# A two-layer attention and expert kernel: attention in two stages, float32r scores over 128 rows, weight splits moved from GpSimd

## Chip, core and metric

The kernel runs on one core of a Trainium2 chip. The metric is device time in microseconds (us) from the start of the program to its end. The engines are named as in the profile: PE is TensorE with its matmuls, PEld its weight loads, DVE is VectorE, ACT is ScalarE, POOL is GpSimd, SP is SyncE, whose queue issues the DMAs.

## What is computed

Two layers over 256 tokens of 1024 features. Layer 0 mixes tokens by a sparse attention with three branches (compressed, selected, window), layer 1 by a forgetting attention with a decay; each is followed by a product-key expert layer. Of the reference, cut to what matters here:

```python
# layer 0 (nsa): 16 heads of 64, 4 key groups; three branches, each gated
q = rope(proj[..., :1024]); k_slc, k_win = rope(kv[:, :, 2]), rope(kv[:, :, 4])
s_c = einsum(q, k_cmp); p_c = masked_softmax(s_c, cmp_end <= t)
s_s = einsum(q, ks);    p_s = masked_softmax(s_s, pos_s <= t)
s_w = einsum(q, kw);    p_w = masked_softmax(s_w, causal window)
o = g0 * (p_c @ v_cmp) + g1 * (p_s @ vs) + g2 * (p_w @ vw);  h = h + o @ w_out
# layer 1 (fox)
s = einsum(q, k) + c[t] - c[k]; p = masked_softmax(s, k <= t); h = h + (p @ v) @ w_out
# after each: h = h + peer_ffn(rms_norm(h)), whose first step is q = x @ w_q
```

With 256 tokens every block is selected and the window covers all, so selected and window attention are both plain causal attention, with keys of their own (branch b = 0, 1 in the kernel).

## The kernel before

A list scheduler sets the order of the instructions on each engine by the data they need and by costs; `pin` keeps a piece in program order, and `tc.issue_after(mark)` holds the ACT instructions written inside it back until ACT has issued the marked one. Each engine then runs its list in order.

Weights come in as float32 and are split into two float32r parts: `hi`, a cast on ACT (L116), and `lo`, a subtract (L117) on DVE or, where `eng` says so, on GpSimd. A projection is three matmuls per block, hi x hi, hi x lo and lo x hi (L200 to L202). `w_half` loads half a weight tile (4 blocks of 128 x 512) into a ring of three slots, by SP (L189); the compression network's weights w1 (L384) use slots of the same ring, so that a slot comes free for the next w_in load when the network's matmuls (L388) that read it are done.

`nsa` is layer 0. It projects the compressed key and value tokens, then k, then q in two tiles of 512 columns (`q_tile`), then v and the gates. k is rotated (`rope`, DVE L291 to L299), transposed on PE (L356) and copied to `kT` by ACT (L358). The token transposes L365 and the DVE adds L370 lay out the input of the compression network, whose matmuls L388 are spread between the matmuls of the q tiles. q is transposed at L430. Then come the compressed scores and softmax (L473 to L490), of which L490 are transposes on PE.

The rounds follow: eight, j = 0 to 7, a round for two heads and two branches. For each half of the tokens (qt) and each of the two heads (s) the scores of both branches go into one PSUM tile: a float32 matmul L508 over 64 rows (256 or 512 columns wide) and a bf16 matmul L509 that adds the causal mask through `identb` and `maskb`. DVE takes the maximum (L510), ACT the exponential (L512), DVE the sums' limit, reciprocal and gate (L513 to L516); the probabilities are scaled on DVE (L523) and ACT (L521), transposed on PE (L529), copied (L532), and multiplied with the values (L539, L540, and L544 for the compressed branch). ACT and DVE split the result (L546, L547), and ACT's cast is kept as `marks[j]`. In the code the values of round j stand right behind its scores.

`fox` is layer 1, with rounds of the same form: scores L641 (66 rows, float32), mask L642, maximum L643, exponential L645, L646 to L649 on DVE, transposes L654, copies L655 and L657, values L662 and L663.

`out_proj` multiplies with w_out in four halves. ACT casts of halves 0, 1 and 2 or 3 are held back to marks 0, 2, 4 (nsa) or 0, 3, 6 (fox); GpSimd subtracts for halves 0 to 2, DVE for half 3. `peer` is the expert layer: the query projection over 16 blocks of wq (`load_split`, L672; matmuls L689, L692, L693), then the long blocks of u and v.

Of the kernel before, what the change touches and what calls it, by code (L numbers as in the profile page):

```python
# [17 lines left out]
P = 128  # L18
S = 256
# [20 lines left out]
def body(ctx, tc, A, out):  # L40
# [12 lines left out]
    identb = const.tile([P, P], BF16, name="identb")  # L53
    maskb = const.tile([P, P], BF16, name="maskb")
# [170 lines left out]
    def out_proj(HL, w, oh, ol, gi, marks):  # L225
# [19 lines left out]
        mm(0, 1)  # L245
        add(0, 0)
        mm(0, 2)
        mm(0, 3)
        add(0, 1)
        mm(1, 1)  # L250
        add(1, 0)
# [8 lines left out]
    def nsa():  # L260
# [3 lines left out]
        TOK, XO, SO = 10240, 12288, 14336  # L264
        qT = ar(6144, 8, S)
        kT = ar(8192, 2, 2, S)
# [76 lines left out]
        for tt in range(2):  # L343
# [3 lines left out]
            for u in range(2):  # L347
                ACT.activation(t4[:, :, u], o[tt][:, 256:512].rearrange("p (g e) -> p g e", e=64), AF.Copy, scale=norm.rs[tt])

        o = proj_tok(HL, wsrc[512], 512, xh, xl)  # L350
        for tt in range(2):
            kf = t2k(4, P)
            rope(o[tt], 8, 1, tt, kf.rearrange("p b (u e) -> p (b u) e", u=2))
            pt = pst("g")
            for b in range(4):
                PE.transpose(pt[:, b * P:(b + 1) * P], kf[:, b], ident)  # L356

            ACT.copy(kT.rearrange("p g b t -> p b g t")[:, :, :, tt * P:(tt + 1) * P],  # L358
                     pt.rearrange("p (b g t) -> p b g t", b=2, g=2))
# [90 lines left out]
        V.reciprocal(gates, gates)  # L450
# [19 lines left out]
        for tt in range(2):  # L470
# [16 lines left out]
            pt = pst("g")  # L487
            pf = ar(XO + tt * 512, 4, P)
# [612 lines left out]
```

## Time and profile before

| | us |
|---|---|
| runs of before | 1962.12, 1963.22, 1964.39 (median 1963.22) |
| profiled execution | 1965.05 |
| its span, first to last instruction | 1962.9 |
| PE busy over the span | 1930.9 |
| DVE busy over the span | 1402.2 |
| ACT busy over the span | 987.4 |
| POOL busy over the span | 158.2 |

The span is 2.15 us shorter than the execution's own time; the rest lies around it. A matmul's busy time is longer than its share of PE, because matmuls overlap: the time from one start to the next is what one costs in a row of them. Layer 0's projections fill the span up to 87.5 us, the compressed softmax to 105.2, the rounds to 167.4, the output projection to 187.8 and the query projection of the expert layer to 240. Layer 1's rounds run from 1075 to 1123 us, its output projection to 1143.

### The profile page before, as it was taken

The page shows a single profiled execution, that of the slowest core. Times are in us where ns is not written, and L with a number is a line of the kernel's source. Part 1 is how long each engine was busy: PE and PEld are TensorE (multiplying, and loading weights), DVE is VectorE, ACT ScalarE, POOL GpSimd, SP SyncE. Part 2 cuts the span into 40 slices and gives each one's busy share as a digit, 9 for nine tenths or more (in the row PEclk, how much of TensorE's full clock was granted, in tenths as well). Part 3 has the DMA queues.
Part 4 walks back from the last instruction along what each step waited for, and adds up shares of the span by engine and source line. Part 5 has one row for each costly group of instructions (what it writes and reads, how often), then busy time and mean ns, then how long its engine had stood idle before and what let it go on. Part 6 is the DMA issues. An engine that isn't in the chain of part 4 may idle for free.

```text
span 1962.9 us, 34000 instructions
## 1 busy us (share of the span) xinstructions
PE 1930.9 (98%) x13091; PEld 1717.4 (87%) x13091; DVE 1402.2 (71%) x2984; ACT 987.4 (50%) x1870; POOL 158.2 (8%) x98
## 2 busy tenths in 40 slices
PE   9999999999999999999999999999999999999998
PEld 6747999999999888888879699999999998888886
DVE  8586998478888655555585779956788875555555
ACT  5564545555444544444463555455544444444444
POOL 4011600000000000000050252000000000000001
PEclk9999999999999999999999799999999999999999
DMA  7701555554545666666664235565454556666664
GB/s 294 262 28 65 162 163 184 181 163 159 157 156 162 223 217 215 192 194 194 194 229 146 70 106 160 174 190 170 159 162 151 162 169 194 194 216 203 194 194 140
DMA packets 90193, 340.91 MB, mean 174 GB/s; under 512 B 9872, under 2 KB 12336, under 8 KB 84656
## 3 DMA queue, kind: packets, MB, share of 16 engines
q1 hardware_dynamic: 89744, 338.22, 54.0%
q8 instruction: 103, 1.69, 0.3%
q10 hardware_dynamic: 288, 0.52, 0.1%
q14 instruction: 58, 0.48, 0.1%
HBM read 334.48 MB, written 4.19 MB: 173 GB/s over the span
## 4 chain that ended last, share of the span: by engine, by line
PE 79%; DVE 15%; ACT 3%; issue 2%; DMA 0%; POOL 0%; ACTq 0%
PE m L966 12%; PE m L965 12%; PE m L964 12%; PE h L692 9%; PE h L689 9%; PE h L693 9%; DVE lo L117 5%; ACT hi L116 2%; PE m L907 2%; PE m L200 2%; PE m L201 2%; PE m L202 2%; PE m L908 1%; PE m L508 1%; DVE vhl L900 1%
## 5 line engine op out<-in xcount | busy, mean ns | idle before, releaser
L117 DVE TENSOR_TENSOR lo<-raw,hi 128x1024 fp32r<-128x1024 f32 x512 | 628.5, 1228 | 397.1 <-ACT hi L116 393.8
L116 ACT CAST hi<-raw 128x1024 fp32r<-128x1024 f32 (+1 forms) x576 | 576.5, 1003 | 640.1 <-PE m L966 293.8
L693 PE MATMUL h<-xh,lo 128*128 128x256 f32 x2048 | 581.8, 284 | 2.1 <-DVE lo L117 2.1
L689 PE MATMUL h<-xh,hi 128*128 128x256 f32 x2048 | 580.6, 284 | 0.9 <-ACT E L925 0.9
L692 PE MATMUL h<-xl,hi 128*128 128x256 f32 x2048 | 580.4, 283 | 0.0
L965 PE MATMUL m<-lo,vhl 128*128 128x512 f32 x1024 | 398.7, 389 | 0.0
L966 PE MATMUL m<-hi,vhl 128*128 128x512 f32 x1024 | 398.7, 389 | 0.0
L964 PE MATMUL m<-hi,vhl 128*128 128x512 f32 x1024 | 398.7, 389 | 0.0
L693 PEld LDWEIGHTS h<-xh,lo 128*128 128x128 f32 x2048 | 386.5, 189 | 4.8 <-DVE lo L117 4.1
L689 PEld LDWEIGHTS h<-xh,hi 128*128 128x128 f32 x2048 | 386.5, 189 | 1.5 <-ACT E L925 1.3
L692 PEld LDWEIGHTS h<-xl,hi 128*128 128x128 f32 x2048 | 386.7, 189 | 0.0
L965 PEld LDWEIGHTS m<-lo,vhl 128*128 128x128 f32 x1024 | 192.4, 188 | 40.3 <-DVE lo L117 0.5
L966 PEld LDWEIGHTS m<-hi,vhl 128*128 128x128 f32 x1024 | 192.4, 188 | 39.9
L964 PEld LDWEIGHTS m<-hi,vhl 128*128 128x128 f32 x1024 | 192.3, 188 | 39.8
L117 POOL TENSOR_TENSOR E<-arena,E 128x1024 fp32r<-128x1024 f32 (+1 forms) x20 | 46.8, 2358 | 917.1 <-ACT E L116 904.0
L117 POOL TENSOR_TENSOR lo<-raw,hi 128x512 fp32r<-128x512 f32 x64 | 90.8, 1438 | 95.6 <-ACT hi L116 95.4
L916 ACT ACTIVATE arena<-m 128x256 f32<-128x256 f32 (+25 forms) x128 | 37.7, 303 | 79.9 <-DVE arena L914 75.9
L116 ACT CAST E<-arena 128x1024 fp32r<-128x1024 f32 (+2 forms) x68 | 62.5, 955 | 27.6 <-DMA arena<-in_w_in 14.4
L689 PE MATMUL h<-E,hi 128*128 128x256 f32 x240 | 70.3, 293 | 3.1 <-ACT arena L761 3.1
L117 DVE TENSOR_TENSOR E<-arena,E 128x1024 fp32r<-128x1024 f32 (+2 forms) x48 | 58.2, 1239 | 17.6 <-ACT E L116 17.5
L117 DVE TENSOR_TENSOR vhl<-E,vhl 128x512 fp32r<-128x512 f32 x64 | 44.1, 688 | 34.1 <-ACT vhl L116 34.1
L693 PE MATMUL h<-E,lo 128*128 128x256 f32 x240 | 68.1, 284 | 0.0
(281 smaller groups left out, 2519.1 us busy)
## 6 DMA issues: line engine op xcount, KB each, us to landing
raw<-in_u SPq DMA_DIRECT2D x256, 512.0 KB, 3.5
raw<-in_v SPq DMA_DIRECT2D x256, 512.0 KB, 3.8
arena<-in_w_in SPq DMA_DIRECT2D x18, 1024.0 KB, 5.0
raw<-in_wq SPq DMA_DIRECT2D x32, 512.0 KB, 3.7
arena<-in_w SPq DMA_DIRECT2D x8, 1024.0 KB, 6.4
arena<-in_w_out SPq DMA_DIRECT2D x8, 1024.0 KB, 5.0
hd<-arena SPq DMA_DIRECT2D x3, 1024.0 KB, 4.5
arena<-hd SPq DMA_DIRECT2D x3, 1024.0 KB, 5.2
```

Source lines behind the costliest of these rows:

```text
L116: ACT.copy(hi, raw)
L117: (eng or V).tensor_tensor(lo, raw, hi.bitcast(F32), ALU.subtract)
L200: PE.matmul(o[:, :n], sh[:, cc, tsl], wh[:, c], start=cc == 0, stop=False)
L201: PE.matmul(o[:, :n], sh[:, cc, tsl], wl[:, c], start=False, stop=False)
L202: PE.matmul(o[:, :n], sl[:, cc, tsl], wh[:, c], start=False, stop=cc == 7)
L689: t = PE.matmul(o[:, :S], hi[:, c % 4], sh[:, c], start=c == 0, stop=False)
L692: PE.matmul(o[:, :S], hi[:, c % 4], sl[:, c], start=False, stop=False)
L693: PE.matmul(o[:, :S], lo[:, c % 4], sh[:, c], start=False, stop=c == 7)
L907: PE.matmul(o, o2[:, k, :, u], oh[:, k, :, u], start=True, stop=False)
L964: PE.matmul(acc[tt][nh], gh[:, ts], vh, start=first, stop=False)
L965: PE.matmul(acc[tt][nh], gh[:, ts], vl, start=False, stop=False)
L966: PE.matmul(acc[tt][nh], gl[:, ts], vh, start=False, stop=last)
```

## The change

Three things change.

Layer 0's scores: `stacked` rotates q or k, splits it into hi and lo, lays both side by side so that a transpose gives 64 rows of hi and 64 of lo, and transposes (8 for each tile of 512 columns and half of the tokens). k is stored twice, hi over hi (`ks_`) and lo over zeros (`kl_`, zeroed by GpSimd), q as hi over lo (`qs_`). A score is then two float32r matmuls over 128 rows and a float32r mask (in fox the mask too). q is also transposed as before, for the compressed branch. These arrays lie in the buffers of the expert layer's weight stream (`ustr`), so that layer 0's wq blocks can't be loaded while they are read. The gates of the rounds are no longer inverted by themselves: one DVE instruction multiplies the limited sum with the gate's denominator, and one reciprocal follows.

Two stages: `weights_of(j)` holds scores, softmax and scaling, `values_of(j)` transposes and values, and round j+1's first is written ahead of round j's second, in both layers. The compressed branch's transposes (`turn_compressed`) stand behind `weights_of(0)`.

Splits: all halves of w_out are split by ACT and DVE, after marks 2, 5, 7; the first two halves' matmuls of both token halves go first. The first two wq blocks are split by ACT and DVE after marks[7], instead of by GpSimd at any time before; the other 14 stay on GpSimd.

```diff
...
-    identb = const.tile([P, P], BF16, name="identb")
-    maskb = const.tile([P, P], BF16, name="maskb")
+    identb = const.tile([P, P], F32R, name="identb")
+    maskb = const.tile([P, P], F32R, name="maskb")
...
-        half_in = lambda i: w_half(HL, w[i // 2][:, i % 2 * 4:i % 2 * 4 + 4, :], 512, (GP, GP) if i < 3 else (V, V))
+        half_in = lambda i: w_half(HL, w[i // 2][:, i % 2 * 4:i % 2 * 4 + 4, :], 512, (V, V))
         ws = []
+        mm = lambda tt, i: proj_mm(o[tt][i // 2], 512, i % 2, tt, oh, ol, *ws[i])
         for i in range(4):
             with tc.issue_after(marks[min(i, 2)]):
                 ws.append(half_in(i))
-            if i == 0:
+            if i < 2:
                 for tt in range(2):
-                    proj_mm(o[tt][0], 512, 0, tt, oh, ol, *ws[0])
+                    mm(tt, i)
...
-        mm(0, 1)
         add(0, 0)
+        add(1, 0)
         mm(0, 2)
         mm(0, 3)
         add(0, 1)
...
+        qs_ = [tl(ustr, t, [4, S], F32R, 3) for t in ("raw", "raw", "raw", "hi")]
+        ks_ = [tl(ustr, "hi", [2, 2, S], F32R, 3) for _ in range(2)]
+        kl_ = [tl(ustr, "lo", [2, 2, S], F32R, 3) for _ in range(2)]
         qT = ar(6144, 8, S)
-        kT = ar(8192, 2, 2, S)
...
+        def stacked(o, ti, tt, put):
+
+            f = t2k(8, 64)
+            rope(o, 8, ti, tt, f)
+            hl = t4k(8, 2, 64)
+            split(f, hl[:, :, 0].bitcast(F32R), hl[:, :, 1])
+            for q in range(2):
+                pt = pst("g")
+                for b in range(4):
+                    PE.transpose(pt[:, b * P:(b + 1) * P], hl[:, 4 * q + b].rearrange("p u e -> p (u e)"), ident)
+                put(q, pt.rearrange("p (b t) -> p b t", b=4))
+            return f
...
+        for x in kl_:
+            GP.memset(x[64:128].bitcast(F32), 0.0)
         o = proj_tok(HL, wsrc[512], 512, xh, xl)
         for tt in range(2):
-            kf = t2k(4, P)
-            rope(o[tt], 8, 1, tt, kf.rearrange("p b (u e) -> p (b u) e", u=2))
-            pt = pst("g")
-            for b in range(4):
-                PE.transpose(pt[:, b * P:(b + 1) * P], kf[:, b], ident)
-
-            ACT.copy(kT.rearrange("p g b t -> p b g t")[:, :, :, tt * P:(tt + 1) * P],
-                     pt.rearrange("p (b g t) -> p b g t", b=2, g=2))
+            def put_k(br, pt):
+                for g01 in range(2):
+                    src = pt[:, 2 * g01:2 * g01 + 2]
+                    to = lambda x: x[:, :, br, tt * P:(tt + 1) * P]
+                    ACT.copy(to(ks_[g01][0:64]), src[0:64])
+                    V.tensor_copy(to(ks_[g01][64:128]), src[0:64])
+                    (ACT.copy if g01 else V.tensor_copy)(to(kl_[g01][0:64]), src[64:128])
+
+            stacked(o[tt], 1, tt, put_k)
...
-                qf = t2k(4, P)
-                rope(o[tt], 8, 0, tt, qf.rearrange("p b (u e) -> p (b u) e", u=2))
+                ts = slice(tt * P, (tt + 1) * P)
+                f = stacked(o[tt], 0, tt, lambda q, pt: ACT.copy(qs_[2 * qi + q][:, :, ts], pt))
+
                 pt = pst("g")
                 for b in range(4):
-                    PE.transpose(pt[:, b * P:(b + 1) * P], qf[:, b], ident)
-                ACT.copy(qT[:, qi * 4:qi * 4 + 4, tt * P:(tt + 1) * P], pt.rearrange("p (b t) -> p b t", b=4))
+                    PE.transpose(pt[:, b * P:(b + 1) * P], f[:, 2 * b:2 * b + 2].rearrange("p u e -> p (u e)"), ident)
+                V.tensor_copy(qT[:, qi * 4:qi * 4 + 4, ts], pt.rearrange("p (b t) -> p b t", b=4))
...
-        V.reciprocal(gates, gates)
+        V.reciprocal(gates[:, :, 0:16], gates[:, :, 0:16])
...
+        def turn_compressed():
+            for tt in range(2):
...
+        def weights_of(j):
             g01, r = j // 4, j % 4
...
-                    PE.matmul(s3, qT[64 * s:64 * s + 64, j, qs], kT[64 * s:64 * s + 64, g01, :, :K], start=True, stop=False)
+                    qx = qs_[2 * g01 + r // 2][:, 2 * (r % 2) + s, qs]
+                    PE.matmul(s3, qx, ks_[g01][:, s, :, :K], start=True, stop=False)
+                    PE.matmul(s3, qx, kl_[g01][:, s, :, :K], start=False, stop=False)
                     PE.matmul(s3[:, :, K - P:K], identb, maskb.unsqueeze(1).broadcast_to((P, 2, P)), start=False, stop=True)
...
-                V.tensor_scalar(su, su, 1e-30, None, ALU.max)
+                gv = gates[:, qt, 16:48].rearrange("p (b r g) -> p g b r", b=2, r=4)[:, g01::2, :, r]
+                V.scalar_tensor_tensor(su, su, 1e-30, gv, ALU.max, ALU.mult)
                 V.reciprocal(su, su)
-                gv = gates[:, qt, 16:48].rearrange("p (b r g) -> p g b r", b=2, r=4)[:, g01::2, :, r]
-                V.tensor_tensor(su, su, gv, ALU.mult)
...
+            return Pts
+
+        def values_of(j, Pts):
+            g01, r = j // 4, j % 4
+            PT0 = ar(TOK + (j % 2) * 1024, 2, 2, S)
+            PT1 = t2k(2, 2, P)
+            for qt, Pt in enumerate(Pts):
...
+        held = weights_of(0)
+        turn_compressed()
+        for j in range(1, 8):
+            nxt = weights_of(j)
+            values_of(j - 1, held)
+            held = nxt
+        values_of(7, held)
         h_in(xsrc)
-        return out_proj(HL, A["w_out0"], oh, ol, 1, [marks[i] for i in (0, 2, 4)])
+        return out_proj(HL, A["w_out0"], oh, ol, 1, [marks[i] for i in (2, 5, 7)]), marks[7]
...
-        return out_proj(HL, A["w_out1"], oh, ol, 3, [marks[i] for i in (0, 3, 6)])
+        return out_proj(HL, A["w_out1"], oh, ol, 3, [marks[i] for i in (2, 5, 7)]), marks[7]
...
-        parts = [load_split(wq[b], (GP, GP)) for b in range(2)]
+        with tc.issue_after(mark):
+            parts = [load_split(wq[b]) for b in range(2)]
...
-    norm = peer(0, nsa())
-    peer(1, fox(norm))
+    norm = peer(0, *nsa())
+    peer(1, *fox(norm))
```

Where the order of instructions moves. On PE, in layer 0's projections, around the token transposes (L365 before, L383 after) and the first compression matmuls (L388, h_463 before; L406, h_511 after); m_432 is a sum of the first q tile, m_629 one of the second, g a PSUM tile of transposes. Before:

```order
L365 MATMUL g_404<-cst,arena 128x128 x2
L388 MATMUL h_463<-arena 15x128 x3
L200 MATMUL m_432<-E_85,xh 128x512
L388 MATMUL h_463<-arena 15x128 x2
L365 MATMUL g_411<-cst,arena 128x128 x2
L388 MATMUL h_463<-arena 15x128 x11
L201 MATMUL m_432<-E_85,xh 128x512
L365 MATMUL g_418<-cst,arena 128x128 x2
L202 MATMUL m_432<-E_85,xl 128x512
L200 MATMUL m_432<-E_85,xh 128x512
```

After:

```order
L406 MATMUL h_511<-arena 15x128 x3
L383 MATMUL g_459<-cst,arena 128x128 x2
L406 MATMUL h_511<-arena 15x128 x11
L383 MATMUL g_466<-cst,arena 128x128 x2
L406 MATMUL h_511<-arena 15x128 x12
L383 MATMUL g_473<-cst,arena 128x128 x2
L406 MATMUL h_511<-arena 15x128 x19
L360 MATMUL g_584<-cst,vhl_581 128x128 x4
L360 MATMUL g_590<-cst,vhl_581 128x128 x4
L200 MATMUL m_629<-E_85,xh 128x512
```

Before, matmuls of the first q tile alternate with both; after, they are all ahead, and the next projection matmul is the second q tile's, behind 8 more transposes of q (L360).

On PE, in layer 0's rounds, the scores (L508 and L509 before; L532, L533 and L534 after), the transposes of the probabilities (L529, L561) and the values (L571). Before:

```order
L508 MATMUL m_1286<-arena 128x512
L509 LDWEIGHTS identb
L509 MATMUL m_1286<-maskb,identb 128x2x128
L508 MATMUL m_1292<-arena 128x512
L529 MATMUL g_1229<-cst,vhl_1207 128x128 x4
L529 MATMUL g_1235<-cst,vhl_1207 128x128 x4
```

After:

```order
L534 MATMUL m_1263<-maskb,identb 128x256
L532 MATMUL m_1270<-hi_90,raw_87 128x256
L533 MATMUL m_1270<-lo_92,raw_87 128x256
L534 MATMUL m_1270<-maskb,identb 128x256
L532 MATMUL m_1286<-hi_90,raw_87 128x512
L533 MATMUL m_1286<-lo_92,raw_87 128x512
L534 MATMUL m_1286<-maskb,identb 128x2x128
L561 MATMUL g_1241<-cst,vhl_1127 128x128 x4
L571 MATMUL h_1247<-arena 64x256
L532 MATMUL m_1293<-hi_90,raw_87 128x512
```

Before, the transposes of g_1229 belong to the round of scores ahead of m_1286 and m_1292 (to m_1210 and m_1216); after, those of g_1241 belong to m_1130 and m_1137, two rounds ahead of m_1286, and each score has two float32r matmuls.

On DVE, in layer 1's rounds, the softmax multiplies (L649 before, L689 after) with sums' limit and reciprocal around them, and the split of a piece of w_out (L117). Before:

```order
L665 TENSOR_TENSOR E_10663<-h_11580,E_10663 128x256
L649 TENSOR_SCALAR vraw_11606<-vraw_11606,fsu_11608 128x256
L647 RECIPROCAL fsu_11637<-fsu_11637 128x2
L646 TENSOR_SCALAR fsu_11655<-fsu_11655 128x2
L646 TENSOR_SCALAR fsu_11684<-fsu_11684 128x2
L649 TENSOR_SCALAR vraw_11635<-vraw_11635,fsu_11637 128x128 x2
L647 RECIPROCAL fsu_11655<-fsu_11655 128x2
L647 RECIPROCAL fsu_11684<-fsu_11684 128x2
```

After:

```order
L689 TENSOR_SCALAR vraw_11749<-vraw_11749,fsu_11751 128x256 x2
L686 TENSOR_SCALAR fsu_11784<-fsu_11784 128x2
L686 TENSOR_SCALAR fsu_11798<-fsu_11798 128x2
L683 TENSOR_REDUCE fnm_11830<-m_11832 128x2
L687 RECIPROCAL fsu_11784<-fsu_11784 128x2
L687 RECIPROCAL fsu_11798<-fsu_11798 128x2
L117 TENSOR_TENSOR E_10783<-arena,E_10783 128x1024
L713 TENSOR_TENSOR E_10783<-h_11775,E_10783 128x256
L689 TENSOR_SCALAR vraw_11782<-vraw_11782,fsu_11784 128x128 x2
L689 TENSOR_SCALAR vraw_11796<-vraw_11796,fsu_11798 128x256 x2
L705 COPY vhl_11810<-g_11815 128x256
L686 TENSOR_SCALAR fsu_11831<-fsu_11831 128x2
```

Before, no split of w_out stands in the piece; after, the first one of that layer stands ahead of the multiplies of sums fsu_11784 and fsu_11798.

## Rows read from the trace of the kernel before

**Rows 1.** Stretch, length; busy us (instructions) by engine; PE's clock; DMA share, GB/s.
```profile
0.00:87.50 87.50, 83.57 (x586) 63.06 (x586) 61.26 (x137) 44.06 (x86) 23.74 (x17) 0.98 0.80 284
105.20:167.40 62.20, 61.47 (x337) 33.17 (x335) 47.10 (x126) 39.39 (x138) 14.04 (x6) 0.97 0.12 39
167.40:187.80 20.40, 20.40 (x98) 16.94 (x97) 10.36 (x31) 7.85 (x21) 0.00 (x0) 1.00 0.16 52
187.80:240.00 52.20, 50.60 (x423) 50.09 (x422) 46.71 (x218) 30.83 (x78) 35.70 (x26) 1.00 0.50 154
...
1075.00:1123.00 48.00, 45.27 (x232) 31.46 (x231) 32.78 (x100) 27.98 (x96) 10.71 (x5) 0.79 0.21 72
```

**Rows 2.** PE's waits in both attentions: engine, line, awaited; us, times, longest.
```profile
PE g L490 <- DVE arena L486: 2.5, 1, 2.5
...
PE g L654 <- DVE vraw L649: 2.7, 2, 2.0
```

**Rows 3.** The same view as rows 1, for layer 1's rounds in pieces.
```profile
1084.00:1092.00 8.00, 6.65 (x41) 4.19 (x39) 7.43 (x21) 5.77 (x18) 3.56 (x2) 1.00 0.45 162
1092.00:1098.00 6.00, 4.65 (x21) 2.75 (x21) 4.71 (x15) 2.41 (x10) 1.15 (x1) 0.75 0.52 176
1098.00:1110.00 12.00, 12.00 (x46) 8.53 (x46) 6.96 (x24) 6.87 (x22) 3.29 (x2) 0.50 0.01 1
1110.00:1116.00 6.00, 5.97 (x22) 3.26 (x18) 4.74 (x13) 3.20 (x13) 1.41 (x1) 0.55 0.50 175
```

**Rows 4.** Timeline of VectorE and GpSimd: start, length, instruction, [idle before <- releaser].
```profile
113.17 2.22 DVE L523 TENSOR_SCALAR vhl<-vhl,su 128x128 f32<-128x128 f32 x1
...
1088.44 4.71 POOL L117 TENSOR_TENSOR E<-arena,E 128x1024 fp32r<-128x1024 f32 x2 [68.89 <-ACT E L116]
1088.46 4.83 DVE L649 TENSOR_SCALAR vraw<-vraw,fsu 128x256 f32<-128x256 f32 x2
...
1096.63 0.61 DVE L649 TENSOR_SCALAR vraw<-vraw,fsu 128x256 f32<-128x256 f32 x2
```

**Rows 5.** Timeline of the first projections, several engines.
```profile
37.85 0.38 PE L365 MATMUL g<-cst,arena 128*128 128x128 f32 x2
44.88 0.33 SPq L189 DMA_DIRECT2D arena<-in_w_in  x1
49.72 1.99 ACT L116 CAST E<-arena 128x1024 fp32r<-128x1024 f32 x2 [9.93 <-DMA arena<-in_w_in]
72.47 1.29 DVE L117 TENSOR_TENSOR E<-arena,E 128x512 fp32r<-128x512 f32 x2 [3.36 <-ACT E L116]
```

**Rows 6.** Timeline of PE in a round of layer 0.
```profile
120.99 1.12 PE L508 MATMUL m<-arena 64*128 64x512 f32 x2
122.04 1.09 PE L529 MATMUL g<-cst,vhl 128*128 128x128 f32 x8
122.97 0.27 PE L509 MATMUL m<-maskb,identb 128*128 128x256 bf16 x1
123.18 0.70 PE L508 MATMUL m<-arena 64*128 64x256 f32 x2
123.80 0.65 PE L539 MATMUL h<-arena 128*64 128x256 f32 x2
```

**Rows 7.** Groups of PE instructions, 105.2 to 167.4 us: count | busy, mean ns.
```profile
L508 PE MATMUL m<-arena 64*128 64x512 f32 x24 | 13.6, 648 | 0.0
...
L508 PE MATMUL m<-arena 64*128 64x256 f32 x20 | 7.0, 428 | 0.0
```

**Rows 8.** Timeline of PE: two projection matmuls in a row.
```profile
24.64 0.40 PE L201 MATMUL m<-E,xh 128*128 128x512 f32 x1
24.87 0.39 PE L202 MATMUL m<-E,xl 128*128 128x512 f32 x1
```

**Rows 9.** Weight loads: one in the timeline, and a group of the page.
```profile
1086.58 0.10 PEld L642 LDWEIGHTS <-identb 128*128 128x128 bf16 x1
...
L689 PEld LDWEIGHTS h<-xh,hi 128*128 128x128 f32 x2048 | 386.5, 189 | 1.5 <-ACT E L925 1.3
```

More of the change, by code (lines that the diff above doesn't have):

```diff
@@ L233, in out_proj @@
                 ws.append(half_in(i))
-            if i == 0:
+            if i < 2:
                 for tt in range(2):
-                    proj_mm(o[tt][0], 512, 0, tt, oh, ol, *ws[0])
+                    mm(tt, i)
         norm = Norm(gi, oh, ol, 12288)
-        mm = lambda tt, i: proj_mm(o[tt][i // 2], 512, i % 2, tt, oh, ol, *ws[i])
         def add(tt, nh):
@@ L249, in out_proj @@
         add(0, 1)
-        mm(1, 1)
-        add(1, 0)
         norm.piece(0, 0)
@@ L486, in nsa @@
             V.tensor_tensor(p3, p3, sm_.unsqueeze(2).broadcast_to((P, 16, 15)), ALU.mult)
-            pt = pst("g")
-            pf = ar(XO + tt * 512, 4, P)
-            for r in range(4):
-                PE.transpose(pt[:, r * P:(r + 1) * P], pf[:, r], ident)
-            V.tensor_copy(pcT[:, :, tt * P:(tt + 1) * P], pt.rearrange("p (r t) -> p r t", r=4))
+        def turn_compressed():
+            for tt in range(2):
+                pt = pst("g")
+                pf = ar(XO + tt * 512, 4, P)
+                for r in range(4):
+                    PE.transpose(pt[:, r * P:(r + 1) * P], pf[:, r], ident)
+                V.tensor_copy(pcT[:, :, tt * P:(tt + 1) * P], pt.rearrange("p (r t) -> p r t", r=4))
         marks = []
-        for j in range(8):
+        def weights_of(j):
             g01, r = j // 4, j % 4
-            PT0 = ar(TOK + (j % 2) * 1024, 2, 2, S)
-            PT1 = t2k(2, 2, P)
+            Pts = []
             for qt in range(2):
@@ L501, in nsa @@
                 qs = slice(qt * P, (qt + 1) * P)
-                Pt = t4k(2, 2, S)
+                Pt = t4k(2, 2, S) if qt else t2k(2, 2, P)
+                Pts.append(Pt)
                 nm = smt("nm", [2, 2], bufs=4)
@@ L523, in nsa @@
                             V.tensor_scalar(x, x, f, None, ALU.mult)
+            return Pts
[4 more added lines that the diff above has]
+            for qt, Pt in enumerate(Pts):
+                qs = slice(qt * P, (qt + 1) * P)
                 for kt in range(qt + 1):
@@ L627, in fox, with weights_of @@
         marks = []
-        for j in range(8):
-            PTt = t4k(768)
-            PT0 = view(PTt[:, :512], (2, S))
-            PT1 = view(PTt[:, 512:], (2, P))
+        def weights_of(j):
+            Pts = []
             for qt in range(2):
@@ L635, in fox @@
                 Pt = t2k(2, S)
+                Pts.append(Pt)
                 nm = smt("fnm", [2], bufs=4)
@@ L649, in fox, with values_of @@
                     V.tensor_scalar(Pt[:, s, :K], Pt[:, s, :K], su[:, s:s + 1], None, ALU.mult)
+            return Pts
+        def values_of(j, Pts):
+            PTt = t4k(768)
+            PT0 = view(PTt[:, :512], (2, S))
+            PT1 = view(PTt[:, 512:], (2, P))
+            for qt, Pt in enumerate(Pts):
+                qs = slice(qt * P, (qt + 1) * P)
                 pt = pst("g")
@@ L665, in fox @@
             V.tensor_tensor(ol[:, j], po[:, :S], oh[:, j].bitcast(F32), ALU.subtract)
+        held = weights_of(0)
+        for j in range(1, 8):
+            nxt = weights_of(j)
+            values_of(j - 1, held)
+            held = nxt
+        values_of(7, held)
         h_in()
-        return out_proj(HL, A["w_out1"], oh, ol, 3, [marks[i] for i in (0, 3, 6)])
+        return out_proj(HL, A["w_out1"], oh, ol, 3, [marks[i] for i in (2, 5, 7)]), marks[7]
     def load_split(src, eng=None):
@@ L694, in feat_block, with peer @@
         return o
-    def peer(li, norm):
+    def peer(li, norm, mark):
         wq, keysd, uT, vd = A[f"wq{li}"], A[f"keys{li}"], A[f"u{li}"], A[f"v{li}"]
```

## The prediction

> **What bounds the kernel now.** I read the busy time by stage first, because the page's average (PE busy nearly all the time) hides stages with different limits. In the first layer's attention rounds PE is busy 61.47 of 62.20 us and VectorE 47.10, so PE sets the pace there; in the first projections PE is busy 83.57 of 87.50, in the output projection 20.40 of 20.40, in the query projection of the expert stage 50.60 of 52.20 [rows 1]. The second layer's attention differs: PE is busy 45.27 of 48.00 us, but its mean clock there is 0.79 [rows 1]. So I read next PE's waits: 2.7 us for the softmax multiply L649 in two pieces, and, in the first layer, 2.5 us in one piece for the compressed softmax [rows 2]. Then the clock: 1.00 until 1092 us, 0.75 for the next 6 us, 0.50 for 12 us and 0.55 for 6 us [rows 3]. The half level (1.2 instead of 2.4 GHz) began right at those waits. Last, what made L649 late: two multiplies that started 0.02 us after GpSimd's first split of w_out took 4.83 us, while a pair of the same shape takes 0.61; in the first layer one multiply of half the width took 2.22 us [rows 4]. GpSimd's split of w_out is therefore not free for VectorE.
>
> **Part A, first projections: a loss.** Splitting k and q into hi and lo doubles the transposes of k (8 more), and each of q's four pieces gets 8 beside its 4: 40 more on PE. Eight take 0.93 us (122.04 to 122.97), 0.116 each [rows 6], so 4.6 us on an engine that has 3.9 us free in the stage. Beside it stands a chain. The token transposes start at 37.85; the first matmuls of the compression network that follow free a ring slot, the next w_in load is issued at 44.88, and ACT, idle for 9.93 us, casts it at 49.72 [rows 5]. The second k tile now stands ahead of the token transposes with a cast (1.99 for two of 1024 columns, so 0.5 for 512) and a subtract (1.29 for two, 0.65), four more transposes (0.46) and more copies (0.3, an estimate): 1.9 us, and 4.2 if one weight piece stands ahead in each of the two queues (1.0 on ACT, 1.3 on VectorE). I take 4. The order shows what is worse: before, 24 matmuls of the first q tile still stood behind the first compression matmul (5.5 us of cover at 0.23 each [rows 8]); now all but one stand ahead of it. So the later load is felt by PE. Bounds: +3 (the chain is hidden and PE's free time takes part of the 4.6) and +10 (4 of delay and 5.5 of lost cover, the extra transposes lying in the gap). I take **+6.5**, the middle, since neither end is nearer to a row.
>
> **Part B, the compressed softmax: +0.5.** VectorE and ACT set this stretch, not PE [rows 2]. Round 2's scores are now issued ahead of it as well, so a few more reductions and exponentials stand in those two queues; the gates' reciprocal gets shorter. Bounds -0.5 and +2.
>
> **Part C, the rounds: the gain.** A score tile of 512 columns is a float32 matmul of 64 rows, 1.05 us (120.99 to 122.04), and of 256 columns 0.62 (123.18 to 123.80); the bf16 mask is 0.21 [rows 6]. The new form is two float32r matmuls, 0.23 each at 512 columns [rows 8], half of it (0.12) at 256, as an estimate, and a mask. The mask's price in float32r isn't in the trace: 0.12 (its 256 columns at the same rate) or 0.21 (as now); I take 0.12, as the projections' matmuls have the same type. That is 1.26 against 0.58 and 0.83 against 0.36. In the rounds there are 24 and 20 records, two to a matmul, so 12 and 10 tiles [rows 7]: 12 x 0.68 + 10 x 0.47 = 12.9 us, and 1.2 for two tiles of round 2 (0.58 each) that move ahead of Part B: 14.1, or 12.1 with the dearer mask. PE would need 47 us.
>
> The mask's identity is now float32r too. Its bf16 weight load takes 0.10 us, the float32 loads of the page 0.19 [rows 9]; the load engine is busy 33.17 of 62.20 us [rows 1], so 20 loads x 0.09 = 1.8 us hide. The Trainium skill, page "TensorE: Matmul & The Clock Gate", section "Weight-path perf modes — Fast Weight Load (FWL) and DoubleRow", says that the fast weight load is on for 128 weights of a type other than FP32, which speaks against this edit; were none of it hidden, Part C would gain 1.8 us less.
>
> VectorE takes GpSimd's splits: two halves of two pieces of 1.3 us [rows 5], 5.2 us. It loses the stretching: six splits on GpSimd took 14.04 us [rows 1], and by the 2.22 us row each holds up VectorE for one to two; I take 7 in all. 47.1 - 7 + 5.2 = 45 us against PE's 47: both near the bound, with waits on each other between. Issuing round j+1's scores ahead of round j's values gives each chain of softmax a round of slack, so I expect 52 us: **-10**, bounds -4 (58, VectorE's chain felt in every round) and -14 (48, PE nearly alone).
>
> **The output projection and the expert stage: 0.** In the first 20.40 us PE has half 0 and half 1 of w_out first, 48 matmuls of 0.23, 11 us; in that time the last two halves' casts and subtracts run (four pieces of 1.0 and 1.3). The two wq blocks' splits that come behind (1.0 on ACT, 1.3 on VectorE each) meet a VectorE that was busy 10.36 us of 20.40 [rows 1] and would be at 15.6. If that cover failed, PE would wait one block, up to 3 us. Blocks 2 and up stay on GpSimd, busy 35.70 of 52.20 us there. The wq loads no longer run among the w_in loads early on; I count nothing for it.
>
> **Second layer's attention: -11.** Without GpSimd's splits the 2.7 us of waits go [rows 2], and with them the slow stretch: 6 us at 0.75, 12 at 0.50, 6 at 0.55 cost 1.5 + 6.0 + 2.7 = 10.2 us over full clock [rows 3]. Together 12.9. VectorE, busy 32.78 of 48.00 with some 7 us of stretching in it, takes 5.2 us of splits; its order above shows the first one between the reciprocals and multiplies of the same round, 1.3 us in the chain. I give 2 back. Bounds -6 (splits delay the rounds, and a part of the slow stretch stays) and -13.
>
> **Sum**: 6.5 + 0.5 - 10 + 0 - 11 = -14. The profiled execution took 1965.05 us, so 1951; the runs' median is 1963.22, 1.8 lower, which I leave inside the range.
>
> **Rivals.** (1) *The clock.* PE, no longer saturated, gets small gaps in both attentions and falls to half as it did at 1092. For it: that fall needed 2.7 us of waits in all. Against it: from 1084 to 1092 PE was busy only 6.65 of 8 us and the clock stayed at 1.00 [rows 3]. A stretch like the 12 us at 0.50 in either attention costs 6, in both 12: 1957 to 1963, I take 1959. The same page of the Trainium skill, section "A second HAM failure mode: psum-queue depth-cycling", tells of a kernel whose PE idled briefly between groups so often that the clock went up and down; the row from 1084 to 1092 doesn't bear that out here. (2) *VectorE becomes the bound*: Part C gives only 4, the second attention 6: 1965 + 7 - 10 = 1962. For it: 45 us of work in 52, and splits inside the softmax chain. (3) *Slower*: the gap in Part A. If PE stands idle the full 10 us ahead of the second q tile, the clock falls there as at 1092, and 12 us at 0.50 cost 6 more: +16, against the 10 us of rival 2 and +0.5 of Part B: 1971. It decides from some 10 us of loss in Part A on, if the rounds gain no more than rival 2 says; the 24 matmuls that leave that place speak for it, the 3.9 us that the stage has free against it.
>
> **Chances and range.** Forecast 0.65 (1940 to 1961 by its bounds), clock 0.13, VectorE 0.14, slower 0.08. A measurement of this kernel can tell about 0.2% (3.9 us) from no change. Faster by more than that, under 1959.3: nearly all of the forecast, half of rival 1, little of rival 2, 0.74. Slower, over 1967.1: rival 3 and the upper end of rival 2, 0.10. Within: 0.16. The range 1940 to 1963 takes in the forecast's bounds and most of rivals 1 and 2.
>
> **What would show it.** Part A right: the first projections' stage longer by 4 to 9 us, with ACT's wait for w_in ending some 4 us later than 49.72. Part C right: two matmuls of 0.23 us a tile, the rounds in 50 to 54 us, PE with waits for VectorE that are shorter than 1 us each. Second attention right: no multiply over 1 us, clock at 1.00 all through, the stage 11 us shorter. Wrong: a clock of 0.50 for over 10 us in either attention (rival 1), VectorE busy over 90% of the rounds and PE under 85% (rival 2), or a first stage longer by 12 us and more (rival 3).

## The result, and the profile after

The changed kernel takes 1952.96 us (median; 1952.18 to 1953.70), the kernel before 1963.73: a ratio of 0.992 with an interval of 0.9891 to 0.9949, 10.8 us faster. The forecast was 1951. Its profiled execution took 1953.70 us, with a span of 1951.9.

By stage (stretch and length; busy us and count by engine; PE's clock; DMA share, GB/s), with stretches that end at the same points of the program as [rows 1], but for 166.0, which lies about 1 us ahead of the end of the rounds, so that rounds and output projection are summed below:

```profile
0.00:97.50 97.50, 86.97 (x625) 67.24 (x626) 71.47 (x156) 48.53 (x96) 14.93 (x13) 0.98 0.64 229
97.50:115.10 17.60, 12.30 (x102) 8.18 (x100) 15.43 (x59) 12.42 (x42) 0.00 (x0) 0.86 0.45 151
115.10:166.00 50.90, 48.90 (x326) 33.63 (x326) 40.09 (x115) 34.84 (x128) 0.00 (x0) 0.95 0.13 42
166.00:187.10 21.10, 21.10 (x103) 17.07 (x101) 14.57 (x34) 12.38 (x27) 4.50 (x2) 1.00 0.52 175
...
1075.00:1115.00 40.00, 40.00 (x242) 28.76 (x242) 29.80 (x104) 25.18 (x94) 0.00 (x0) 1.00 0.26 86
```

The reader is to see two things. Layer 0's first projections are 10 us longer (97.5 against 87.5), its rounds and output projection 10.5 us shorter (72.0 us from 115.1 to 187.1, against 82.5 from 105.2 to 187.8). So the whole of layer 0's attention ends 0.7 us earlier, at 187.1: the cheaper scores pay for their own preparation and no more. And layer 1's rounds run at a clock of 1.00 with PE busy all the time, where [rows 3] had 0.75, 0.50 and 0.55. From layer 1's first score (1077.9 before, 1077.1 after) to its first query matmul (1143.1, 1131.4) is 65.2 us before and 54.3 after: 10.9 us, and the spans differ by 11.0.

PE's waits, in the first two stretches of layer 0 after the projections and in layer 1:

```profile
PE m L532 <- ACT vhl L537: 2.3, 4, 1.3
PE g L416 <- ACT arena L412: 1.3, 1, 1.3
...
PE g L150 <- DVE arena L1050: 3.4, 1, 3.4
PE h L744 <- ACT arena L817: 1.5, 1, 1.5
```

The wait for the softmax multiply (L649 in [rows 2], L689 now) is gone; the last two rows lie ahead of and behind layer 1's attention and were there before. The multiplies take 347 ns on average, as the undisturbed pair of [rows 4] did (0.61 us for two), and VectorE now has the splits (groups of layer 1's rounds, 1075 to 1115 us; count | busy, mean ns):

```profile
L689 DVE TENSOR_SCALAR vraw<-vraw,fsu 128x256 f32<-128x256 f32 x16 | 4.9, 347 | 0.0
L117 DVE TENSOR_TENSOR E<-arena,E 128x1024 fp32r<-128x1024 f32 x4 | 4.9, 1213 | 0.6 <-ACT E L116 0.4
```

Of the 22 executions of the kernel of e5 and e10 below, ten took 1970 to 1982 us at a mean granted clock of 0.979 to 0.985 and the others 1952 to 1957 at 0.993 to 0.995; the five of over 1981 are left out of its ratios, the other five are in them, and no trace of any of the ten was kept.

### The profile page after: what moved, and what is told of

The parts are those of the page before. It is cut to its first block, busy times and chain, and to the rows that moved or that the text cites. A ratio compares the mean times of both kernels' runs of the same rounds, so it can differ in the third digit from the quotient of the medians.

```text
span 1951.9 us, 34088 instructions
## 1 busy us (share of the span) xinstructions
PE 1913.0 (98%) x13131; PEld 1718.6 (88%) x13131; DVE 1411.2 (72%) x3006; ACT 994.0 (51%) x1886; POOL 120.5 (6%) x80
## 3 DMA queue, kind: packets, MB, share of 16 engines
q1 hardware_dynamic: 89744, 338.22, 54.6%
## 4 chain that ended last, share of the span: by engine, by line
PE 76%; DVE 15%; ACT 4%; issue 2%; DMA 1%; POOL 0%; SPq 0%; ACTq 0%; DVEq 0%
PE m L1021 12%; PE m L1022 12%; PE m L1020 12%; PE h L747 8%; PE h L744 8%; PE h L748 8%; DVE lo L117 5%; ACT hi L116 3%; PE m L963 2%; PE m L200 2%; PE m L202 2%; PE m L201 2%; PE m L964 1%; DVE vhl L956 1%; DVE vraw L955 1%
## 5 line engine op out<-in xcount | busy, mean ns | idle before, releaser
L117 DVE TENSOR_TENSOR lo<-raw,hi 128x1024 fp32r<-128x1024 f32 x516 | 634.9, 1231 | 397.9 <-ACT hi L116 394.3
L117 POOL TENSOR_TENSOR lo<-raw,hi 128x512 fp32r<-128x512 f32 x56 | 79.4, 1438 | 242.4 <-ACT hi L116 242.3
L972 ACT ACTIVATE arena<-m 128x256 f32<-128x256 f32 (+25 forms) x128 | 37.6, 303 | 79.9 <-DVE arena L970 75.9
L117 DVE TENSOR_TENSOR E<-arena,E 128x1024 fp32r<-128x1024 f32 (+2 forms) x60 | 70.8, 1208 | 10.1 <-ACT E L116 9.7
L117 DVE TENSOR_TENSOR vhl<-E,vhl 128x512 fp32r<-128x512 f32 x64 | 44.1, 688 | 34.1 <-ACT vhl L116 34.1
L963 PE MATMUL m<-vhl 128*128 128x128 f16 x512 | 65.4, 218 | 2.7 <-DVE vhl L956 0.2
```

What stands on the lines that cost most here:

```text
L117: (eng or V).tensor_tensor(lo, raw, hi.bitcast(F32), ALU.subtract)
L963: PE.matmul(o, o2[:, k, :, u], oh[:, k, :, u], start=True, stop=False)
```

## Experiments

The points of the program that the verdicts use, in us from the span's start, each from the first or last instruction of a line (tok: first token transpose; turned: last transpose of the compressed branch; q0: first query matmul of layer 0's expert stage; s1 and q1: first score of layer 1, last matmul of its output projection):

| kernel | tok | turned | q0 | s1 | q1 | span | ratio to before (interval) |
|---|---|---|---|---|---|---|---|
| before | 37.8 | 105.0 | 187.8 | 1077.9 | 1142.9 | 1962.9 | 1 |
| changed | 47.3 | 115.1 | 187.1 | 1077.1 | 1131.1 | 1951.9 | 0.992 (0.9891 to 0.9949) |
| e0 changed, again | 48.5 | 115.3 | 187.1 | 1077.1 | 1131.1 | 1951.6 | 0.9925 (0.9899 to 0.9951) |
| e1 splits on GpSimd | 46.9 | 114.6 | 187.0 | 1077.0 | 1134.2 | 1954.3 | 0.9955 (0.9939 to 0.9972) |
| e2 one stage | 47.6 | 112.6 | 198.2 | 1087.1 | 1140.6 | 1960.9 | 0.9991 (0.9979 to 1.0003) |
| e3 old scores | 36.6 | 104.3 | 185.6 | 1076.3 | 1130.3 | 1950.9 | 0.9941 (0.9924 to 0.9957) |
| e4 tokens first | 24.5 | 109.8 | 183.6 | 1075.0 | 1129.0 | 1949.9 | 0.992 (0.9903 to 0.9936) |
| e5 before, splits on VectorE | 37.3 | 105.6 | 188.8 | 1079.6 | 1134.1 | 1954.4 | 0.9954 (0.9907 to 1.0002) |
| e10 the kernel of e5, again | 37.7 | 104.9 | 188.0 | 1078.7 | 1133.3 | 1953.1 | 0.9959 (0.9918 to 1.0) |
| e6 tokens first, late turn | 24.5 | 116.5 | 184.3 | 1075.4 | 1129.4 | 1949.1 | 0.9904 (0.9875 to 0.9933) |
| e7 before, two stages | 37.6 | 106.1 | 195.8 | 1085.6 | 1147.2 | 1967.0 | 0.9972 (0.9946 to 0.9999) |
| e8 tokens first, copies on ACT | 25.2 | 112.7 | 185.1 | 1075.3 | 1129.3 | 1950.1 | 0.9907 (0.987 to 0.9944) |
| e9 e8 with late turn | 25.2 | 119.5 | 187.3 | 1078.2 | 1132.2 | 1953.7 | 0.9916 (0.9887 to 0.9945) |
| e11 old scores, late turn | 37.5 | 109.9 | 183.7 | 1073.3 | 1127.3 | 1947.6 | 0.9892 (0.9857 to 0.9927) |

The kernel before had a median of 1966 to 1968 us beside these runs, so ratios are compared, and spans within a stage. e0 only repeats the changed kernel:

> The changed kernel itself, beside the runs that follow. All theories: 0.992 of the kernel before, 8 to 13 us below it.

It did: 0.9925.

### e1: the splits back on GpSimd

```diff
-        half_in = lambda i: w_half(..., 512, (V, V))
+        half_in = lambda i: w_half(..., 512, (GP, GP) if i < 3 else (V, V))
```

> The changed kernel, with the subtracts of w_out's halves 0 to 2 on GpSimd again; marks, order of the matmuls, scores and two stages stay. Theory A (the splits on GpSimd hold up VectorE's softmax multiplies, and the waits that follow cost PE its full clock): multiplies of 2 to 5 us come back beside the splits, layer 1's rounds take 6 to 12 us more and layer 0's 1 to 4 more: 1958 to 1968 us against 1953. Theory B (two stages give layer 1 its 11 us, because a late multiply has a round of slack): multiplies of 2 to 5 us come back, PE doesn't wait for them for over 1 us in all: 1951 to 1956 us.

Layer 1 takes 57.2 us from s1 to q1 instead of 54.0, layer 0 the same. PE's waits in layer 1:

```profile
PE h L711 <- DVE vhl L705: 2.0, 2, 1.1
PE g L702 <- DVE vraw L689: 1.2, 1, 1.2
```

A stretch in which some of them fall:

```profile
1110.00:1116.00 6.00, 4.29 (x26) 2.96 (x27) 3.77 (x7) 1.47 (x4) 2.29 (x1) 1.00 0.42 147
```

The group of the multiplies, 1077 to 1134 us:

```profile
L689 DVE TENSOR_SCALAR vraw<-vraw,fsu 128x256 f32<-128x256 f32 x16 | 8.4, 568 | 0.0
```

The multiplies are held up again (568 ns on average against 347), PE waits 3.2 us in all, and the clock stays at 1.00 all the same. So with two stages and the later marks GpSimd's splits cost 3.1 us, not the 11 of the kernel before: neither theory's number, B the nearer in mechanism. What is missing here is the slow clock, 10.2 of the 12.9 us in the prediction's sum. Whether the second stage or the later marks keep it away isn't shown: no run changes the marks alone, and with two stages and the old marks (e7) it was at 0.50 from 1104 to 1110 us.

### e2: one stage

```diff
-        for j in range(1, 8):
-            nxt = weights_of(j)
-            values_of(j - 1, held)
-            held = nxt
-        values_of(7, held)
+        values_of(0, held)
+        for j in range(1, 8):
+            values_of(j, weights_of(j))
```

> The changed kernel, with each round's values written right behind its own scores again, in both layers; the splits stay on VectorE. Theory A (the splits' place gives layer 1 its gain): layer 1's rounds keep 8 to 11 of their 11 us, 1953 to 1957 us in all, since the scheduler issued scores a round ahead before, too. Theory B (two stages give it): layer 1's rounds lose 6 us and more, PE waits for L689's multiplies: 1959 to 1967 us.

Layer 1 is as theory A has it: 53.5 us from s1 to q1, no slower than with two stages. The total isn't, since layer 0 loses 11 us, which neither theory had; its time of 1964.26 us lies in theory B's range for that other reason. PE's waits there:

```profile
PE g L561 <- DVE vhl L547: 7.3, 6, 1.2
...
PE h L571 <- DVE arena L564: 4.4, 6, 1.1
```

Two stretches of its rounds:

```profile
130.00:140.00 10.00, 7.34 (x52) 5.17 (x52) 7.50 (x22) 7.90 (x29) 0.00 (x0) 1.00 0.17 55
140.00:150.00 10.00, 7.65 (x45) 5.80 (x46) 7.48 (x20) 6.23 (x27) 0.00 (x0) 0.83 0.49 157
```

PE is busy 73 and 77% of them, VectorE 75%: neither is the bound, the chain from score to value is. The clock, 0.83 from 140 to 160 us, costs at most 3.4 of the 11 us. With float32 scores PE's own time covered that chain; with the cheap ones only the second stage does.

### e3: layer 0's scores as before

```diff
-                    PE.matmul(s3, qx, ks_[g01][:, s, :, :K], start=True, stop=False)
-                    PE.matmul(s3, qx, kl_[g01][:, s, :, :K], start=False, stop=False)
+                    PE.matmul(s3, qT[64 * s:64 * s + 64, j, qs], kT[64 * s:64 * s + 64, g01, :, :K], start=True, stop=False)
```

with `stacked`, `qs_`, `ks_` and `kl_` gone and `identb`, `maskb` in bf16 again.

> The changed kernel, with layer 0's scores as before: float32 over 64 rows, bf16 mask, k and q neither split nor stacked; two stages and splits as in the change. Theory A (in layer 0 the cheaper scores pay 10 us in the rounds and the split and stacked k and q cost 10 us in the first projections): the first projections end near 88 us instead of 97.5, the rounds take 6 to 11 us longer, the first query projection starts within 3 us of 187: 1950 to 1957 us in all. Theory B (the projections' 10 us come from something else, the moved wq loads or the order of the ring): the projections stay at 95 us or more and the rounds get longer: 1960 to 1966 us.

Theory A: the token transposes start at 36.6 us, the compressed branch is turned at 104.3 (10.8 earlier than in the changed kernel), the last projection matmul starts at 85.9 (97.4 in the changed kernel), and the rounds give all but 1.5 us back: q0 is at 185.6 against 187.1.

```profile
L722 PE MATMUL h<-E,hi x240: 276/283/384, 185.6 to 1185.1; 128*128 128x256 f32 x120
```

By the times the two can't be told apart (0.9941 and 0.992, intervals that overlap). The float32r scores, the largest part of the diff, are worth nothing as they stand.

### e4: token transposes ahead of k

```diff
+        for kv in range(2):
+            for g in range(4):
+                ...
         for x in kl_:
             GP.memset(x[64:128].bitcast(F32), 0.0)
         o = proj_tok(HL, wsrc[512], 512, xh, xl)
         ...
-        for kv in range(2):
-            for g in range(4):
-                ...
```

> The changed kernel, with the token transposes and the adds that lay out the compression network's input written ahead of the k projection instead of behind it. Theory A (the 10 us in the first projections come from k's second tile, whose split, 8 transposes and 12 copies stand ahead of the token transposes, so that the ring slot for the second q tile's weights comes free 8.6 us later): that w_in load is issued at 45 us or earlier instead of 53.4, the projections end at 89 to 94 us, 1944 to 1950 us in all. Theory B (they come from PE's 40 more transposes and VectorE's extra splits as such): the projections end at 96 us or later, 1951 to 1954 us.

The compressed branch is turned at 109.8 us, 5.3 earlier than in the changed kernel, and q0 comes at 183.6, 3.5 earlier; 2.0 us of that are left at the end of the span. The w_in load that the changed kernel issues at 53.4 us is issued at 37.3, and the last projection matmul starts at 93.8 instead of 97.4, the first as theory A has it, the second at the upper end of its range. So 3.5 us of the 10 at the projections' end, and 5.3 behind the compressed softmax, came from the order of k and the token transposes; the rest is what k's and q's splitting adds, by the difference to e3. The time (1950.95, beside runs of the kernel before at 1966) lies between the theories' ranges, and its ratio is that of the changed kernel, 0.992: the gain shows in the trace alone.

### e5 and e10: the kernel before, with the splits on VectorE alone

```diff
-        half_in = lambda i: w_half(..., 512, (GP, GP) if i < 3 else (V, V))
+        half_in = lambda i: w_half(..., 512, (V, V))
```

> The kernel before, with one edit: GpSimd splits none of w_out (all subtracts on VectorE); marks and order of the matmuls as before. Theory A (the splits on GpSimd alone cause layer 1's waits and its slow stretch): layer 1's rounds are 9 to 12 us shorter at a clock of 1.00; layer 0's rounds, where PE set the pace, within 2 us: 9 to 13 us below the kernel before. Theory B (the waits come from the order of the rounds, and without two stages VectorE's own splits make them too): 0 to 5 us below it.

> The kernel before with the one edit that GpSimd splits none of w_out, once more, in more rounds: 7 to 11 us below the kernel before if its trace (8.5 us shorter in its span) is what the times show; within 3 us of it if the slow runs seen beside it are the rule.

Layer 1 takes 54.6 us from s1 to q1 in both traces, against 65.0 before and 54.0 in the changed kernel: 10.4 of its 10.9 us, from one edit. Two stretches of its rounds in e5:

```profile
1090.00:1100.00 10.00, 10.00 (x67) 7.20 (x67) 8.43 (x31) 6.86 (x26) 0.00 (x0) 1.00 0.23 94
1100.00:1110.00 10.00, 9.46 (x54) 6.13 (x53) 8.37 (x28) 8.76 (x31) 0.00 (x0) 1.00 0.32 106
```

Clock 1.00, PE never waiting for a multiply. Layer 0 loses 1.0 us in e5, the expert stage 0.7. Theory A for layer 1. The ratios (0.9954 and 0.9959) have intervals that reach 1. The traced executions are 8.5 and 9.8 us shorter in their spans, as e10's first expectation has it; its median of all executions, 1970.42, lies 3.0 us above that of the kernel before (1967.45), at the edge of its second. The times can't show how much the edit is worth in the mean. So the traces show what GpSimd's splits do in layer 1, and not that this edit by itself makes the kernel faster.

### e7: the kernel before, with two stages alone

The code of the rounds as in the change, scores, splits on GpSimd and marks as before.

> The kernel before, with one edit: values of a round written behind the next round's scores, in both layers; scores, splits on GpSimd and marks as before. Theory A (in layer 1 two stages or the splits' place alone each suffice against the slow stretch; in layer 0, with float32 scores, PE sets the pace anyway): layer 1's rounds 6 to 9 us shorter, layer 0's within 2: 5 to 10 us below the kernel before. Theory B (two stages pay only with the cheaper scores and the splits on VectorE): within 3 us of the kernel before.

The median is 0.5 us below that of the kernel before, which is theory B's number. The trace has neither theory's parts: layer 1's attention is 3.4 us shorter, and layer 0's ends 8.0 later. The traced execution (1969.12) is the longest of its runs (1957.32 to 1969.12), so its clock is one case of several. In layer 0's rounds, GpSimd's splits, a multiply beside the second and a wait of PE in the timeline:

```profile
117.72 2.36 POOL L117 TENSOR_TENSOR E<-arena,E 128x1024 fp32r<-128x1024 f32 x1 [48.91 <-ACT E L116]
122.41 2.36 POOL L117 TENSOR_TENSOR E<-arena,E 128x1024 fp32r<-128x1024 f32 x1 [2.33 <-ACT E L116]
...
122.50 2.35 DVE L528 TENSOR_SCALAR vraw<-vraw,su 128x128 f32<-128x128 f32 x1
...
126.82 0.65 PE L552 MATMUL h<-arena 128*64 128x256 f32 x2 [1.66 <-DVE arena L545]
```

The stretches of that wait and behind it:

```profile
125.00:135.00 10.00, 8.34 (x31) 3.51 (x30) 6.39 (x22) 5.47 (x20) 0.89 (x1) 0.70 0.32 105
135.00:145.00 10.00, 10.00 (x32) 5.37 (x33) 4.22 (x11) 4.45 (x15) 3.85 (x2) 0.50 0.00 0
```

This is the mechanism of layer 1 in [rows 3] once more, in another place: VectorE late beside GpSimd's splits, PE idle for 1.66 us, then ten us at 0.50 with PE busy all the time. In this execution, then, two stages alone move the stall and don't remove it; the fastest (1957.32) may have gone without it, but has no trace.

### e6, e8, e9, e11: towards a better version

e6 is e4 with the compressed branch's transposes inside the first round's values, e8 is e4 with all copies of the transposed k and q on ACT, e9 has both, e11 is e3 with e6's edit:

```diff
         held = weights_of(0)
-        turn_compressed()
...
+            if j == 0:
+                turn_compressed()
             for s in range(2):
                 rows = slice(64 * s, 64 * s + 64)
                 g = g01 + 2 * s
                 PE.matmul(po[rows, :S], vc[32 * g:32 * g + 15, :], pcT[32 * g:32 * g + 15, r, :], ...
```

> The kernel with the token transposes ahead of k, and the compressed branch's transposes written inside the first round's values, behind that round's other transposes and matmuls. Theory A (PE stands still for 4.5 us ahead of those transposes with work of the rounds ready, and its clock falls for it): PE's longest wait there falls under 2 us, the stretch at half clock goes, the rounds end 3 to 6 us earlier: 3 to 6 us below the kernel with the token transposes first. Theory B (VectorE and ACT, both busy with the softmax in that stretch, set it): the rounds end within 1.5 us of where they did.

> The kernel with the token transposes ahead of k, and all copies of the transposed k and q (12 of 64 x 256 and 4 of 128 x 512) on ACT instead of partly on VectorE. Theory A (in the first projections VectorE is now the bound, busy 9.5 of 10 us from 20 to 40 and 50 to 60 us): 5 to 8 us less on VectorE there, PE's waits for its splits (2.8 us) go, the first query projection starts 2 to 5 us earlier than 183.6. Theory B (what is left of the loss is PE's own, 4.6 us of transposes): it starts within 1 us of 183.6.

> The same with the compressed branch's transposes inside the first round's values too. Theory A (they add up): up to 1 us under the kernel without that second edit, 1944 to 1949 us where the kernel before takes 1963. Theory B (the later transposes only move the wait): within 1 us of it, or above.

> Layer 0's scores as before the change (float32 over 64 rows, nothing split or stacked), two stages and the splits as in the change, and the compressed branch's transposes inside the first round's values. Theory A (PE, which sets the pace of the rounds with these scores, stands still ahead of those transposes only because the rounds' own stand behind them): its 1.9 us wait goes and the clock stays up through 105 to 115 us, where it was 0.73; the first query projection starts 3 to 5 us earlier than 185.6, 1946 to 1951 us in all where the kernel before takes 1963 to 1966, without the cheaper scores. Theory B (VectorE and ACT are late for these transposes, too): within 1.5 us of 185.6, 1951 to 1955.

In e6 the wait ahead of those transposes (3.4 us in e4) goes and two others come, so that q0 is at 184.3 instead of 183.6, and the clock from 110 to 120 us is 0.68: theory B.

```profile
PE m L532 <- ACT vhl L537: 2.9, 6, 1.6
PE g L561 <- DVE vhl L547: 2.1, 2, 1.9
```

In e8 VectorE's load falls as meant, from 9.52 to 5.01 us between 50 and 60 us (e4, then e8), and q0 comes later, at 185.1:

```profile
50.00:60.00 10.00, 9.71 (x73) 7.50 (x66) 9.52 (x18) 4.45 (x10) 0.00 (x0) 1.00 0.76 297
50.00:60.00 10.00, 8.27 (x69) 6.11 (x68) 5.01 (x11) 6.86 (x18) 0.00 (x0) 1.00 0.85 315
```

PE's waits for VectorE's splits, 2.8 us in e4 for those of the weights, are 2.4 for these and 2.2 for q's (0.2 in e4), up to 190 us. So VectorE's load between 50 and 60 us wasn't the bound that theory A took it for; what is, these runs leave open. e9 doesn't add up: q0 at 187.3, 1954.05 us, though its ratio (0.9916) can't be told from e8's (0.9907). In e11, with the float32 scores, the wait goes (1.9 us in e3), a longer one takes its place, and q0 still comes 1.9 us earlier than in e3, about half of what theory A has; the clock from 105 to 115 us is 0.77 (0.73 in e3), not up as it has it:

```profile
PE m L511 <- ACT vhl L515: 3.6, 1, 3.6
```

e11 is the fastest of all, 1950.21 us, ratio 0.9892 (0.9857 to 0.9927), span 1947.6; e6 comes next by the ratio (0.9904). Both are under the changed kernel's span by 2.5 us and more; by the intervals of the ratios alone neither is apart from it. e11 does without stacked k and q, without the float32r scores and without the buffers they take.

## Why the prediction was right, point by point

The total came out at -11 of -14 us, in the range; the 3 us that are missing are nearly all Part A's. The terms:

| term | forecast | measured | from |
|---|---|---|---|
| Part A, first projections | +6.5 (+3 to +10) | +10.0 | 87.5 to 97.5 |
| Part B, compressed softmax | +0.5 | -0.1 | 17.7 to 17.6 |
| Part C, rounds, with output projection | -10 | -10.5 | 82.5 to 72.0 |
| layer 1's attention, with output projection | -11 | -10.9 | 65.2 to 54.3 |
| the rest | 0 | +0.5 | what is left to the spans' -11.0 |

**Part A** was mis-sized, too short by 3.5 us, and its path was right only in part. The step that failed is "I take 4" for the delay of the token transposes; they start at 47.30 instead of 37.85, 9.4 us later, and the next w_in load follows at 53.43 instead of 44.88, 8.6 later. PE's first token transposes, the load and its cast (which waited only 0.46 us for it):

```profile
47.30 0.44 PE L383 MATMUL g<-cst,arena 128*128 128x128 f32 x2
...
53.43 3.09 SPq L189 DMA_DIRECT2D arena<-in_w_in  x3
...
58.55 1.99 ACT L116 CAST E<-arena 128x1024 fp32r<-128x1024 f32 x2 [0.46 <-DMA arena<-in_w_in]
```

The chain that ended last shows why (time, length, what):

```profile
40.44 0.69 DVE vraw L297
41.17 0.42 DVE hi L374
41.62 1.23 DVE E L117
42.84 0.61 DVE vhl L117
43.59 0.64 PE g L360 x4
44.25 0.37 ACT hi L373
44.65 0.42 DVE hi L374
45.08 0.43 DVE lo L375
...
47.60 0.42 DVE hi L374
48.05 0.46 DVE arena L388 x2
...
55.47 0.48 DVE arena L388 x2
55.96 0.42 DVE vhl L294
...
58.13 0.70 DVE vhl L117
58.97 1.94 PE g L360 x8
```

From 36 to 59 us it is nearly all VectorE. The copies of k's first tile (L374, L375) stand between the pieces of the second tile's rotation, which ends with L297, and a weight split (1.23) stands ahead of k's own split; the estimate had the second tile's work alone, and one piece of each queue. The lost cover was as described: after the last first-tile matmul PE has only the compression network, then waits 2.85 us, until 58.97. But what it waits for is a split of q, whose rotation stands behind all of the adds L388 in VectorE's queue, and not the late load, which Part A had as the path. In e4 that load is issued 16 us earlier and the projections end only 3.5 us earlier. That the bound of +10 held is luck: it is 4 us of delay and 5.5 of lost cover, and with the 8.6 us measured for the load the same addition gives 14. Of the 10.0 us, 3.4 are PE's own work (86.97 us busy, 83.57 before) and 6.6 its idle time (10.53, 3.93 before).

**Part C** came out where it was put, for the reason given, though at a lower clock than forecast: 0.95 in the rounds. The prices hold: from 149.63 on, a float32r matmul of 512 columns takes 0.23 us to the next start, the mask 0.12, the lower of the two values (first row: the mask's weight load):

```profile
149.63 0.19 PEld L534 LDWEIGHTS m<-maskb,identb 128*128 128x128 f32 x1
...
149.63 0.39 PE L533 MATMUL m<-lo,hi 128*128 128x512 f32 x1
149.86 0.28 PE L534 MATMUL m<-maskb,identb 128*128 128x256 f32 x1
149.98 0.60 PE L561 MATMUL g<-cst,vhl 128*128 128x128 f32 x4
```

The mask's weight load takes 0.19 us where it took 0.10 in bf16 [rows 9]. This agrees with the rule that the prediction cites from the Trainium skill, page "TensorE: Matmul & The Clock Gate", section "Weight-path perf modes — Fast Weight Load (FWL) and DoubleRow", that the fast weight load is on for types other than FP32. It costs nothing in this row: the next start comes after 0.12 us. VectorE lost its stretching, 7 us in the estimate: multiplies of 128 columns, 18 in the rounds, took 11.6 us before and 4.1 after, 7.5 less:

```profile
L523 DVE TENSOR_SCALAR vhl<-vhl,su 128x128 f32<-128x128 f32 x18 | 11.6, 686 | 0.1
...
L547 DVE TENSOR_SCALAR vraw<-vraw,su 128x128 f32<-128x128 f32 x18 | 4.1, 281 | 0.1
```

That the second stage carries this gain was right, and stronger than written: without it (e2) layer 0's attention ends 11 us later.

**Layer 1** was right in size and in cause, and the two traces of e5 and e10 show the cause by itself: with the splits off GpSimd, and nothing else, the waits and the slow stretch go. The second stage isn't needed for it in the traces (e2: 53.5 us with one stage). The 2 us given back for VectorE's splits are not to be told from 0 or 3 (12.9 estimated as lost, 10.9 gained).

**The rivals.** The clock (1) was at 0.50 in layer 0 from 110 to 120 us, 5 us of it in the rounds, where the kernel before had some 7 us of it in all (from the means of 0.90 and 0.97 in its two stretches, an estimate): the prediction's sign for this rival, over 10 us, was just reached, at a cost of under 2 us more than before; in layer 1 it stayed at 1.00; VectorE (2) did not become the bound, with 40.09 of 50.90 us in the rounds; Part A (3) reached the 10 us from which that rival decides, but the rounds gave their full gain. From q0 to s1, over the expert stage, both kernels take 890 us, as written.

## What to carry to other kernels

Price a preparation against the stage it serves: here 10 us saved in the rounds cost 10 us ahead of them, on a chain through another engine, and no profile of the rounds alone shows that. A split on an idle engine isn't free when it holds up the engine that feeds PE: a short late piece there can cost PE its clock for far longer than the piece. And an engine made cheaper needs work issued ahead, or the chain behind it sets the pace.

## What the runs showed of the hardware that was not expected

A few us of waits cost 10 us and more of half clock in one case and nothing in another. In [rows 2 and 3] 2.7 us of waits are followed by 12 us at 0.50 with PE busy 12.00 of 12.00; in e7 one wait of 1.66 us by ten us at 0.50 with PE busy all of them. In e1 waits of 3.2 us, part of them in a stretch in which PE is busy 4.29 of 6.00 us, went at 1.00; in e2 ten us with PE busy 73% went at 1.00 and the next ten, with 77%, at 0.83. What tells these cases apart the runs don't show.

GpSimd's splits don't slow VectorE evenly: they hold up single operations until the split ends, whatever their size. In e1, of the 16 limits of the sums, 128 x 2, 14 take 0.14 to 0.17 us, and two, which start while a split runs, 0.92 and 1.54:

```profile
1102.64 2.43 POOL L117 TENSOR_TENSOR E<-arena,E 128x1024 fp32r<-128x1024 f32 x1 [5.41 <-ACT E L116]
...
1102.89 0.42 DVE L713 TENSOR_TENSOR E<-h,E 128x256 fp32r<-128x256 f32 x1
1103.47 0.42 DVE L705 COPY vhl<-g 128x256 f32<-128x256 f32 x1 [0.16 <-ACT vhl L703]
1104.18 0.92 DVE L686 TENSOR_SCALAR fsu<-fsu 128x2 f32<-128x2 f32 x1 [0.28 <-ACT vraw L685]
```

The limit that starts at 1104.18 ends at 1105.10, the split at 1105.07. The long multiplies of [rows 4] end in the same way: the one of 113.17 at 115.39, 0.09 us behind a split that ended at 115.30. The add L713 and the copy L705, which read the PSUM tiles h and g, took their usual 0.42 us beside the same split. So in these traces the cost depends on which operation of VectorE happens to start while a split runs.
